# A layer pair with eight experts on one core: every expert ranked by load, none loaded ahead of the router

## The chip, the cores and the metric

The kernel runs on one core of one Trainium2 chip. The metric is the time of one launch on the device, in microseconds (us). The kernel before took 1318.35 us in the median of three runs (1315.09 to 1318.83). A profile is one further execution with the hardware profiler on; its span runs from the first to the last instruction.

## The reference, cut to what matters

Two layers are applied to 256 tokens of 1024 numbers (fp32): a mixer layer with a dense feed-forward, and a convolution layer with eight experts, of which each token takes two. Only the experts concern the change:

```python
def swiglu(u, w1, w3, w2):
    return (jax.nn.silu(u @ w1) * (u @ w3)) @ w2

logits = tokens @ router_w                    # 256 tokens, 8 experts
top_vals, top_idx = lax.top_k(logits, 2)
gates = jax.nn.softmax(top_vals, axis=-1)
# token by token: y = sum over its 2 experts e of gates[e] * swiglu(u, w1[e], w3[e], w2[e])
#   w1[e], w3[e]: 1024 x 2816, w2[e]: 2816 x 1024
x = x + gt_f * rmsnorm(y, ffn_post_g)
```

An expert's three matrices are 34.6 MB in fp32, all eight 277 MB. Each has to be read once, however few tokens its expert gets; how many it gets is known only when the router has run.

## The kernel before, in words

**Units.** All weights lie in memory as blocks of 128 x 2048 fp32 numbers, 1.05 MB each (a unit). An expert has 33: for each of five blocks of 512 hidden columns (j = 0 to 4) two units of w1, two of w3 and two of w2, and for the last 256 columns (j = 5) one of each. Eight experts have 264. A unit's key is `(name, expert, j, h)`; the same unit of the next expert lies `NU` = 33 further on. SP issues one transfer for a unit (or one for each half), and a transfer waits until the buffer that it goes to is free.

**Buffers.** The list `room` (L1557 to L1564) says, unit by unit, which buffers a unit goes to: six named `raw`, four pairs `whi`/`wlo`, one pair `gp`/`m`, three or four named `B`. A unit that goes to `whi`/`wlo` is one fp32 half in each; during a 128-slot expert these buffers hold something else (below), and the list goes round ten units instead of fifteen.

**Slots.** The token columns of an expert are gathered into slots by a one-hot matrix on TensorE (`Group.onehot`, `Group.gather`). How many slots an expert has is fixed when the program is built; which expert gets them is found at run time. The first turn is expert 0 with 96 slots (`FIRST`), and its addresses are known when the program is built. The other seven are ranked by their number of tokens (`ranks`, L1990), and rank r has `SLOTS[r]` slots out of 128, 96, 96, 96, 64, 64, 32. `TURNS` gives the order of work. So the slots of the eight turns are

| turn | 0 | 1 | 2 | 3 | 4 | 5 | 6 | 7 |
|---|---|---|---|---|---|---|---|---|
| before | 96 (expert 0) | 32 | 96 | 96 | 64 | 96 | 128 | 64 |

For the ranked ones SP reads the expert's base address from the tile `bases` into a register (L2054), and the transfers add it to a unit's place. An expert with more tokens than slots is finished in a loop after the last turn (`overflow`), whose count is also made in `ranks`.

**An expert's work.** For each j: `up` makes x·w1 and x·w3, `act` the gated product, `turn` transposes it on TensorE, and `down` multiplies by w2 into two PSUM banks; the downs of j - 1 stand behind the ups of j. With 128 slots (`Expert`) each weight half is split into a rounded and a remainder part (L372 on ACT, L373 on DVE, into the four `whi` and four `wlo`), and a product takes three matmuls of 128 x 512 in fp32r. With fewer (`Tiled`) fp32 weights are used as they are: a 64-slot pass puts two products side by side in TensorE's columns, a 32-slot pass four. 96 slots are one pass of each, and the units of w1 and w3 of one j stay in their buffers until the second pass is done. The last expert's result is scaled by its gates (`slot_gate`) and added on TensorE, the others on DVE.

**What sets the order.** From the last norm of the convolution layer on (L1707) the order of TensorE, DVE and ACT is that of the code (`in_order`). The list `todo` holds the expert steps; what stands in `due` (L2181 to L2218) is worked in between them: the rest of expert 0's gather, gates, ranks, and the one-hot and gather of the next group (`GROUPS`), which the turn before it carries. SP keeps the order in which loads are asked for, up to `AHEAD` steps ahead in the code and as far ahead in time as buffers allow. `warm(n)` is n matmuls whose result nobody reads.

**Steps ahead of the experts.** Norms, the transposes `turned` (L1718, L1721), the router's product `logits`, its two best per token `top2`, the places within an expert `slots` (a matmul with a triangle), `Group(0)`'s one-hot, the split token rows `parts` (L1598, L1599) and half of the first gather (L1748). Three units of expert 0 are asked for earlier still (L1542).

Of the kernel before, what the change touches and what calls it, by code (L numbers as in the profile page):

```python
# [236 lines left out]
def build(ctx: ExitStack, tc: tile.TileContext, d, unit, dbg=None):  # L237
# [1363 lines left out]
    def slots(t):  # L1601
# [5 lines left out]
        return lambda: V.tensor_copy(pos[:, t], pp[:, :NE])  # L1607

    def onehot(dst, iota_eq, selc):
        V.tensor_scalar(dst, K("iota"), iota_eq, selc, ALU.is_equal, ALU.mult)  # L1610

    def gather(Os, parts, hi_copy=A.copy, kps=range(KT // 2), bank="aux"):
# [4 lines left out]
        for kp in kps:  # L1617
# [6 lines left out]
            for a, b, dst in parts:  # L1624
# [5 lines left out]
                if len(dst) == 2:  # L1630
                    hi, lo = (x[:, 2 * kp : 2 * kp + 2] for x in dst)
                    hi_copy(hi, v)
                    V.tensor_tensor(lo, v, f(hi), ALU.subtract)
        return (i,)

    class Group:
# [61 lines left out]
    def slots_of(i):  # L1698
        return FIRST if TURNS[i] is None else SLOTS[TURNS[i]]
# [5 lines left out]
    place = {0: (lambda t: pos[:, t, 0:1], lambda t: sel[:, t, 0:1])}  # L1705

    with in_order():  # L1707
# [17 lines left out]
        A.copy(xT_[:, 4:8, P:], b1[1])  # L1725
        logits(0)
# [21 lines left out]
        i = g0.gather(range(2))  # L1748
# [86 lines left out]
    class Tiled(Expert):  # L1835
# [94 lines left out]
        def parts(self, g=None):  # L1930
# [3 lines left out]
            for on, p_, w, n in ((self.A, self.yp[0], 512, 1), (self.B, self.yp[1], T, 2)):  # L1934
# [37 lines left out]
    posr, selr, gtr = (tl([P, TT, NE - 1], n) for n in ("posr", "selr", "gtr"))  # L1972
    r7 = [tl([P, NE - 1, NE - 1], "r7", bufs=4) for _ in range(2)]
    bases = tl([P, NE - 1], "bases", I32)

    posv, selv, gtv = (tl([P, TT, 2 * NE], n) for n in ("posv", "selv", "gtv"))
    blocks = tl([P, 3, 8], "blocks", I32)

    def by_rank(dst, src):

        for t in range(TT):
            x = tl([P, NE - 1, NE - 1], "r7", bufs=4)
            G.tensor_tensor(x, r7[1], src[:, t, 1:].unsqueeze(1).to_broadcast([P, NE - 1, NE - 1]), ALU.mult)
            V.tensor_reduce(dst[:, t], x, AX.X, ALU.add)

# [4 lines left out]
    def ranks():  # L1990

        pcnt = pm("aux")
        for t in range(TT):
            mm(pcnt[:, 0:8], one, sel[:, t, :], t == 0, t == TT - 1)
        cnt, key = tl([P, NE], "cnt"), tl([P, NE], "key")
        A.copy(cnt, pcnt[:, 0:8])

        G.tensor_scalar(key, cnt, float(NE), None, ALU.mult)
        G.tensor_tensor(key, key, K("iota8"), ALU.subtract)
        sq = [P, NE - 1, NE - 1]  # L2000
        V.tensor_tensor(r7[0], key[:, 1:].unsqueeze(1).to_broadcast(sq), key[:, 1:].unsqueeze(2).to_broadcast(sq), ALU.is_gt)
        rank = tl([P, NE - 1], "rank")
        V.tensor_reduce(rank, r7[0], AX.X, ALU.add)
        i7 = K("iota8")[:, : NE - 1]
        V.tensor_tensor(r7[1], rank.unsqueeze(1).to_broadcast(sq), i7.unsqueeze(2).to_broadcast(sq), ALU.is_equal)
        x = tl(sq, "r7", bufs=4)
        G.tensor_tensor(x, r7[1], K("iota8")[:, 1:].unsqueeze(1).to_broadcast(sq), ALU.mult)
        b = tl([P, NE - 1], "bf")
        V.tensor_reduce(b, x, AX.X, ALU.add)
        V.tensor_scalar(bases, b, float(NU), None, ALU.mult)  # L2010
        by_rank(posr, pos)
        by_rank(selr, sel)

        cap = tl([P, NE], "cap")
        G.memset(cap, float(FIRST))
        G.memset(cap[:, 1:], float(P))
        for r in range(1, NE - 1):
            if SLOTS[r] != SLOTS[r - 1]:
                x = tl([P, NE - 1], "capx", bufs=2)
                V.tensor_scalar(x, rank, float(r), float(SLOTS[r - 1] - SLOTS[r]), ALU.is_ge, ALU.mult)  # L2020
                G.tensor_tensor(cap[:, 1:], cap[:, 1:], x, ALU.subtract)
        more = tl([P, 2 * NE], "more")
# [17 lines left out]
        V.tensor_copy(key, ti)  # L2040
        V.tensor_copy(blocks[:, 0], key)
        V.tensor_scalar(cnt, key, float(NE), float(NE), ALU.is_ge, ALU.mult)
        V.tensor_tensor(key, key, cnt, ALU.subtract)
        V.tensor_scalar(blocks[:, 1], key, float(NU), None, ALU.mult)
        V.tensor_scalar(top, top, 0.0, None, ALU.is_gt)
        V.tensor_reduce(key[:, 0:1], top, AX.X, ALU.add)
        V.tensor_copy(blocks[:, 2, 0:1], key[:, 0:1])

    base = []

    def at_base():

        for r in range(NE - 1):
            base.append(nc.values_load(bases[0:1, r : r + 1], engines=(ET.SP,), min_val=NU, max_val=(NE - 1) * NU))  # L2054
# [5 lines left out]
    sums_, gs = [], tl([P, 1], "gs")  # L2060
# [261 lines left out]
```

## Time and profile before

| what | us |
|---|---|
| median of three runs | 1318.35 |
| lowest, highest | 1315.09, 1318.83 |
| the profiled execution | 1315.59 |
| its span | 1313.5 |
| router's last choice written | 595.46 |
| first matmul of an expert starts | 604.62 |
| last matmul of the last expert ends | 1297.45 |

The profiled execution is 2.1 us longer than its span; the rest is launch. Times below count from the span's start. The experts take 693 of the 1313 us. In the tables of stretches, a stretch's columns are its length, then for each engine the busy time and the number of instructions, TensorE's granted clock (1.00 is 2.4 GHz, 0.50 is 1.2 GHz), the mean busy share of the DMA engines, and what they moved in GB/s. A busy TensorE is one with a matmul under way, at whatever clock.

### The profile page before, as it was taken

Reading aid. Unit: us, or ns where it says so; the run is one execution under the profiler, and the core shown is the slowest. Engines: PE = TensorE matmul, PEld = TensorE weight load, DVE = VectorE, ACT = ScalarE, POOL = GpSimd, SP = SyncE. Lnnn points to the kernel's source line nnn. Section 1 sums busy time; section 2 is a strip of 40 time slices with the busy share of each in tenths; the row PEclk is TensorE's granted clock in tenths of the full one; section 3 lists DMA queues with packets and bytes.
Section 4 is the critical chain, followed back from the end, with each engine's and each line's share of the span. In section 5 each row is a group of like instructions: output and inputs, shape, how many; then the busy total and the mean of one; then the engine's idle time right before and its main releaser. Section 6 shows DMA issues by size and latency. Waiting matters only on the chain. (4 is left out here: it accounts for less than half of the span.)

```text
span 1313.5 us, 22646 instructions
## 1 busy us (share of the span) xinstructions
PE 1249.1 (95%) x9212; PEld 803.6 (61%) x9212; DVE 641.1 (49%) x1065; ACT 439.2 (33%) x800; POOL 32.4 (2%) x83
## 2 busy tenths in 40 slices
PE   6999999989999998998999889999999999999996
PEld 5878777789998987675344333443433434678532
DVE  4589758698887658663202112011121121699422
ACT  4553246564434554253012000210011102577311
POOL 1000001100000010002000000000000000000000
PEclk8999999999999999987899889999999999999998
DMA  8727720478988616677679999999999996999994
GB/s 337 284 94 304 299 122 1 160 299 349 370 320 328 256 66 198 195 273 300 238 277 398 419 419 420 420 422 396 368 417 419 419 400 270 423 357 375 351 420 193
DMA packets 71090, 406.42 MB, mean 309 GB/s; under 512 B 7874, under 2 KB 12226, under 8 KB 31812
## 3 DMA queue, kind: packets, MB, share of 16 engines
q1 hardware_dynamic: 70980, 404.91, 78.8%
q8 instruction: 74, 1.21, 0.4%
q14 instruction: 36, 0.29, 0.1%
HBM read 402.94 MB, written 1.93 MB: 308 GB/s over the span
## 5 line engine op out<-in xcount | busy, mean ns | idle before, releaser
L373 DVE TENSOR_TENSOR wlo<-raw,whi 128x1024 fp32r<-128x1024 f32 x154 | 185.8, 1221 | 47.4 <-ACT whi L372 46.5
L282 PE MATMUL mm<-raw,gL 128*32 128x256 f32 (+3 forms) x1392 | 194.3, 438 | 5.1 <-DMA raw<-w 5.1
L372 ACT CAST whi<-raw 128x1024 fp32r<-128x1024 f32 x154 | 159.1, 1049 | 97.1 <-PE mm L282 61.2
L282 PE MATMUL mm<-B,whi 128*128 128x256 f32 x960 | 172.0, 282 | 0.2 <-issue 0.2
L282 PEld LDWEIGHTS mm<-B,whi 128*128 128x128 f32 x960 | 148.6, 189 | 2.3 <-issue 1.0
L282 PE MATMUL mm<-B,wlo 128*128 128x256 f32 x480 | 135.0, 281 | 0.0
L282 PE MATMUL mm<-B,gL 128*32 128x256 f32 (+3 forms) x808 | 124.4, 449 | 3.3 <-DMA B<-w 3.3
L282 PEld LDWEIGHTS mm<-raw,gL 128*32 128x32 f32 (+1 forms) x1392 | 76.8, 122 | 82.7 <-issue 57.3
L1887 DVE TENSOR_TENSOR cv<-cv,mm 64x512 f32<-64x512 f32 (+1 forms) x36 | 23.3, 647 | 189.9 <-ACT cv L1886 189.7
L1886 ACT ACTIVATE cv<-mm 64x512 f32<-64x512 f32 (+1 forms) x36 | 19.9, 553 | 268.1 <-PE mm L282 268.0
L282 PE MATMUL aux<-whi,pT 128*128 128x512 f32 (+2 forms) x400 | 100.9, 425 | 2.4 <-DVE pT L1903 1.8
L282 PEld LDWEIGHTS mm<-B,wlo 128*128 128x128 f32 x480 | 90.7, 189 | 0.0
L282 PEld LDWEIGHTS mm<-B,gL 128*32 128x32 f32 (+1 forms) x808 | 46.7, 123 | 55.4 <-issue 41.3
L282 PE MATMUL aux<-raw,pT 128*32 128x256 f32 (+1 forms) x592 | 77.9, 470 | 0.8 <-DMA raw<-w 0.8
L282 PE MATMUL aux<-wlo,pT 128*32 128x256 f32 (+2 forms) x284 | 69.4, 430 | 2.0 <-DVE wlo L373 1.1
L1903 DVE COPY pT<-aux 128x384 f32<-128x384 f32 (+4 forms) x42 | 19.0, 453 | 100.2 <-PE aux L1896 91.5
L282 PEld LDWEIGHTS aux<-whi,pT 128*128 128x128 f32 (+2 forms) x400 | 49.4, 158 | 27.3 <-issue 13.0
L282 PE MATMUL mm<-U,whi 128*128 128x256 f32 (+1 forms) x240 | 64.5, 331 | 0.0
L282 PE MATMUL aux<-B,pT 128*32 128x256 f32 (+2 forms) x424 | 59.7, 467 | 0.0
L282 PE MATMUL mm<-whi,gL 128*32 128x256 f32 (+3 forms) x336 | 55.9, 452 | 2.3 <-DMA whi<-w 2.3
L282 PE MATMUL mm<-whi,B 128*128 128x512 f32 (+1 forms) x192 | 57.9, 377 | 0.0
L282 PE MATMUL mm<-wlo,gL 128*32 128x256 f32 (+3 forms) x336 | 53.9, 445 | 0.2 <-DMA wlo<-w 0.2
(467 smaller groups left out, 1875.3 us busy)
## 6 DMA issues: line engine op xcount, KB each, us to landing
raw<-w SPq DMA_DIRECT2D x237, 1024.0 KB, 7.3
B<-w SPq DMA_DIRECT2D x69, 1024.0 KB, 11.2
whi<-w SPq DMA_DIRECT2D x52, 512.0 KB, 11.3
wlo<-w SPq DMA_DIRECT2D x52, 512.0 KB, 11.4
gp<-w SPq DMA_DIRECT2D x18, 512.0 KB, 10.0
m<-w SPq DMA_DIRECT2D x18, 512.0 KB, 10.0
B<-hd SPq DMA_DIRECT2D x24, 142.0 KB, 5.3
x<-x SPq DMA_DIRECT2D x2, 512.0 KB, 4.5
```

What stands on the lines that cost most here:

```text
L282: PE.matmul(out, lhsT, rhs, start=start, stop=stop)
L372: A.copy(hi, rq)
L373: V.tensor_tensor(lo, rq, f(hi), ALU.subtract)
L1886: A.activation(s, p_[:64, :w], AF.Silu)
L1887: V.tensor_tensor(s, s, p_[64:, :w], ALU.mult)
L1903: V.tensor_copy(h[:, :o], pt[:, :o])
```

## The change

All eight experts are ranked, and the slots of the eight turns become

| turn | 0 | 1 | 2 | 3 | 4 | 5 | 6 | 7 |
|---|---|---|---|---|---|---|---|---|
| after | 128 | 96 | 64 | 96 | 64 | 96 | 64 | 32 |

640 slots instead of 672: one 96 has become a 64. No unit of an expert is asked for before the bases are known. The count of tokens (`counted`) and the ranking (`ranks`) move from the first expert's work to the router, between `top2` and the gather; the ranking is done by MAX8 and FIND_INDEX8 instead of comparisons, and the sorted places come from one product and one sum over both token halves (`by_rank`). The part that counts leftovers is split (`too_many`, `left`) and stands later. Unselected tokens are now left out by place 0 instead of by a factor. 20 warm matmuls are added between the router's steps. The first four steps' units are loaded in two halves. The rounded part of the first gather is copied by DVE instead of ACT. Cut to its core:

```diff
-FIRST = 96
-SLOTS = (128, 96, 96, 96, 64, 64, 32)
-TURNS = (None, 6, 1, 2, 4, 3, 0, 5)
-GROUPS = ((0,), (1, 2), (3, 4), (5,), (6, 7))
+SLOTS = (128, 96, 96, 96, 64, 64, 64, 32)
+TURNS = (0, 1, 4, 2, 5, 3, 6, 7)
+GROUPS = ((0,), (1, 2), (3, 4), (5, 6), (7,))
...
-            if j:
-                for k in (("m1", 0, 0, 0), ("m3", 0, 0, 0), ("m1", 0, 0, 1)):
-                    pre[k] = raw(k)
...
-    room += ["raw"] * 3 + ["pT"] + ["w"] * 4 + ["xn", "gp"] + ["B8"] * 4
-    while asked() < whole - 30:
-        room += ["raw"] * 6 + ["w"] * 4 + ["gp"] + ["B8"] * 4
-    while asked() < whole + NU + 8:
-        room += ["raw"] * 6 + ["gp"] + ["B8"] * 3
-    while asked() < NU * NE - 13:
+    while len(room) < NU + 8:
+        room += ["raw"] * 6 + ["gp"] + ["B8"] * 3
+    while len(room) < NU * (NE - 1) - 6:
+        room += ["raw"] * 6 + ["w"] * 4 + ["gp"] + ["B8"] * 4
+    while len(room) < NU * NE - 13:
         room += ["raw"] * 6 + ["w"] * 4 + ["B8"] * 3
...
+    def counted():
+        pc = pm("mm")
+        for t in range(TT):
+            mm(pc[:, :NE], one, sel[:, t], t == 0, t == TT - 1)
+        return pc
+
+    def ranks(pc):
+
+        V.scalar_tensor_tensor(ckey, pc[:, :NE], float(NE), K("iota8"), ALU.mult, ALU.subtract)
+        V.max(top, ckey)
+        V.max_index(ti, top, ckey)
+        V.tensor_copy(tif, ti)
+        V.tensor_scalar(bases, tif, float(NU), None, ALU.mult)
+        V.tensor_tensor(r8, tif.unsqueeze(2).to_broadcast(sq), K("iota8").unsqueeze(1).to_broadcast(sq), ALU.is_equal)
...
+        warm(6)
         b0 = turned(xt[:, 0])
...
+        warm(3)
         b1 = turned(N.w[1])
...
+        warm(3)
         logits(0)
...
+        warm(2)
         logits(1)
...
+        warm(4)
         p0 = slots(0)
         top2(1, r1, ry)
+        warm(2)
+        pc = counted()
         p1 = slots(1)
+        ranks(pc)
...
-        i = g0.gather(range(2))
+        i = g0.gather(range(2), V.tensor_copy)
...
-            later(0, partial(g0.gather, (2, 3)))
-            later(1, gates, ranks)
-            later(2, g0.turn)
-            later(3, first)
+            later(2, *[partial(g0.gather, (k,), V.tensor_copy) for k in (2, 3)])
+            later(5, g0.turn)
+            later(7, gates, first, partial(by_rank, gtr, gt))
+            later(10, too_many)
+            later(30, left)
...
-                        if q == 0:
-                            r = raw(sk, src and src())
-                        halves_[key, q] = r[q] if few(key[1]) else half(r, q)
+                    if q == 0:
+                        r = raw(None, unit_of(key[1], key[0], *key[2:]), two=n < 4)
+                    halves_[key, q] = r[q] if few(key[1]) else half(r, q)
```

On SP, before, the first address is read (TENSOR_LOAD) behind 22 units of the first expert; the last of these are

```order
L347 DMA B_1131_6218<-w 128x2048
L347 DMA B_1132_6220<-w 128x2048
L347 DMA B_1169_6502<-w 128x2048
L347 DMA raw_6229<-w 128x2048
L347 DMA raw_6261<-w 128x2048
L347 DMA raw_6286<-w 128x2048
L347 DMA raw_6288<-w 128x2048
L2054 TENSOR_LOAD bases_5835
L2054 ISA x2
L347 DMA raw_1146_6336<-w 128x2048
```

On SP, of the change, it stands right behind the convolution's shifted rows (B from hd), ahead of every expert unit:

```order
L1347 DMA B_884_4576<-hd_5217 32x4x284 x4
L1347 DMA B_885_4577<-hd_5275 32x4x284 x4
L2049 TENSOR_LOAD bases_5682
L2049 ISA x2
L344 ISA
L344 DMA raw_5900<-w 128x1024
L344 ISA
L344 DMA raw_5900<-w 128x1024
L344 ISA
L344 DMA raw_5911<-w 128x1024
```

What moved is the address load: from behind 22 units of the experts to ahead of the first.

On DVE, before, from the router's last choice (sel) to the remainder of the token rows (B from x):

```order
L1594 SCALAR_TENSOR_TENSOR sel_5673<-cst_66,ixf_5678,s_1001_5672 128x8
L1607 COPY pos_5675<-mm_5776 128x8
L1663 TENSOR_SCALAR oh_5791<-cst_66,pos_5675,sel_5673 128x128 x2
L1599 SCALAR_TENSOR_TENSOR B_999_5670<-x_64,rs_1042_5738,B_998_5669 128x512
L1607 COPY pos_5675<-mm_5785 128x8
L1663 TENSOR_SCALAR oh_5791<-cst_66,pos_5675,sel_5673 128x128 x2
L1599 SCALAR_TENSOR_TENSOR B_999_5670<-x_64,rs_1048_5768,B_998_5669 128x512
```

On DVE, of the change, from the same choice to the first of these remainders:

```order
L1587 SCALAR_TENSOR_TENSOR sel_5667<-cst_66,ixf_5672,s_998_5666 128x8
L1714 SCALAR_TENSOR_TENSOR key_5681<-mm_5815,cst_66 128x8
L1715 MAX top_5678<-key_5681 128x8
L1716 MAX_INDEX ti_5679<-top_5678,key_5681 128x8
L1717 CAST tif_5680<-ti_5679 128x8
L1718 TENSOR_SCALAR bases_5682<-tif_5680 128x8
L1719 TENSOR_TENSOR r_1014_5683<-tif_5680,cst_66 128x64
L1601 SCALAR_TENSOR_TENSOR pos_5669<-mm_5803,sel_5667 128x8
L1601 SCALAR_TENSOR_TENSOR pos_5669<-mm_5818,sel_5667 128x8
L1725 TENSOR_TENSOR r8x_5833<-r_1014_5683,pos_5669 128x128
L1726 TENSOR_REDUCE posr_5684<-r8x_5833 128x16
L1608 TENSOR_SCALAR oh_5830<-iota_1008_5676,posr_5684 128x128
```

The ranking, ten instructions, now stands between the choice and the one-hot.

On PE, before, the router's matmuls stand back to back (aux: transposes; mm from rwg: logits):

```order
L575 MATMUL aux_5711<-cst_66,x_64 128x128 x4
L575 MATMUL aux_5716<-cst_66,x_64 128x128 x4
L575 MATMUL aux_5726<-cst_66,xn_5685 128x128 x4
L575 MATMUL aux_5731<-cst_66,xn_5685 128x128 x4
L282 MATMUL mm_5680<-rwg_5372,B_997_5668 128x8 x8
L282 MATMUL mm_5681<-rwg_5372,B_997_5668 128x8 x8
L282 MATMUL mm_5776<-sel_5673,cst_66 128x8
```

On PE, of the change, the warm matmuls (from identr) stand between them, and the count (sel, one) behind the places of the first half:

```order
L281 MATMUL mm_5715<-identr_522 128x512 x6
L574 MATMUL aux_5722<-cst_66,x_64 128x128 x4
L574 MATMUL aux_5727<-cst_66,x_64 128x128 x4
L281 MATMUL mm_5737<-identr_522 128x512 x3
L574 MATMUL aux_5741<-cst_66,xn_5689 128x128 x4
L574 MATMUL aux_5746<-cst_66,xn_5689 128x128 x4
L281 MATMUL mm_5758<-identr_522 128x512 x3
L281 MATMUL mm_5674<-rwg_5372,B_994_5662 128x8 x8
L281 MATMUL mm_5777<-identr_522 128x512 x2
L281 MATMUL mm_5675<-rwg_5372,B_994_5662 128x8 x8
L281 MATMUL mm_5798<-identr_522 128x512 x4
```

Fourteen of the warm ones stand ahead of the second half's logits, six more ahead of the count.

## Rows read from the trace of the kernel before

**Rows 1.** The page's busy times: engine, us, share of the span, instructions.

```profile
PE 1249.1 (95%) x9212; PEld 803.6 (61%) x9212; DVE 641.1 (49%) x1065; ACT 439.2 (33%) x800; POOL 32.4 (2%) x83
```

**Rows 2.** Stretches: router with loads ahead, then one row an expert, then the end.

```profile
544.00:600.00 56.00, 52.41 (x356) 41.59 (x355) 35.21 (x90) 25.14 (x55) 4.01 (x9) 0.88 0.83 284
600.00:701.45 101.45, 96.21 (x806) 44.10 (x810) 15.20 (x55) 16.78 (x41) 5.50 (x28) 0.93 0.71 276
701.45:761.65 60.20, 49.35 (x675) 24.75 (x677) 10.88 (x23) 5.55 (x13) 0.00 (x0) 0.89 1.02 421
761.65:860.01 98.36, 94.92 (x827) 40.67 (x823) 15.19 (x31) 13.09 (x33) 0.00 (x0) 0.98 1.02 419
860.01:954.65 94.64, 94.64 (x885) 39.13 (x887) 15.58 (x28) 8.49 (x18) 0.00 (x0) 1.00 0.98 394
954.65:1027.94 73.29, 73.29 (x461) 29.32 (x461) 14.00 (x27) 10.21 (x22) 0.00 (x0) 1.00 1.02 419
1027.94:1121.83 93.89, 93.89 (x804) 39.61 (x804) 16.03 (x31) 14.07 (x35) 0.00 (x0) 1.00 0.89 360
1121.83:1221.99 100.16, 99.52 (x549) 76.27 (x547) 86.91 (x85) 73.55 (x82) 0.00 (x0) 1.00 0.97 378
1221.99:1291.72 69.73, 69.16 (x341) 29.02 (x341) 17.85 (x26) 11.25 (x20) 0.00 (x0) 1.00 0.98 398
```

**Rows 3.** Timeline of ACT: activations of the last column block, first and last expert.

```profile
701.45 0.38 ACT L1886 ACTIVATE cv<-mm 64x256 f32<-64x256 f32 x1 [7.40 <-PE mm L282]
...
1291.72 0.38 ACT L1886 ACTIVATE cv<-mm 64x256 f32<-64x256 f32 x1 [7.37 <-PE mm L282]
```

**Rows 4.** Timeline of SP: the last loads ahead, and the next ones.

```profile
591.87 3.55 SPq L347 DMA_DIRECT2D B<-w  x5
615.00 20.70 SPq L347 DMA_DIRECT2D raw<-w  x6
```

**Rows 5.** Timeline of PE and DVE in the router and at the first expert.

```profile
581.51 6.32 PE L282 MATMUL aux<-B,B 128*128 128x512 f32 x27
595.23 0.23 DVE L1594 SCALAR_TENSOR_TENSOR sel<-cst,ixf,s 128x8 f32<-128x8 f32 x1
595.57 0.60 DVE L1663 TENSOR_SCALAR oh<-cst,pos,sel 128x128 fp32r<-128x128 f32 x2
595.97 0.57 PE L282 MATMUL mm<-sel,one 128*128 128x8 f32 x2
597.47 2.07 DVE L1599 SCALAR_TENSOR_TENSOR B<-x,rs,B 128x512 fp32r<-128x512 f32 x3
604.62 12.08 PE L282 MATMUL mm<-raw,gL 128*64 128x512 f32 x96
```

**Rows 6.** Timeline of DVE: MAX8 to the cast of what it found.

```profile
623.97 0.18 DVE L2038 MAX8 top<-more 128x8 f32<-128x16 f32 x1 [3.04 <-POOL more L2035]
624.46 0.17 DVE L2040 CAST key<-ti 128x8 f32<-128x8 uint32 x1
```

**Rows 7.** The address loads, and a stretch behind the load issued at 615.00.

```profile
L2054 SPq TENSOR_LOAD <-bases x7: 262/265/459, 619.7 to 661.3; - x7
...
617.00:618.00 1.00, 1.00 (x9) 0.69 (x10) 0.00 (x0) 0.39 (x2) 0.38 (x2) 1.00 1.00 401
```

**Rows 8.** The page's group of remainder subtractions on DVE.

```profile
L373 DVE TENSOR_TENSOR wlo<-raw,whi 128x1024 fp32r<-128x1024 f32 x154 | 185.8, 1221 | 47.4 <-ACT whi L372 46.5
```

**Rows 9.** Timeline of PE: two w2 units at 64 slots, then the end.

```profile
1282.88 3.60 PE L282 MATMUL aux<-raw,pT 128*64 128x512 f32 x16
1293.60 3.85 PE L282 MATMUL aux<-raw,pT 128*64 128x512 f32 x16
```

**Rows 10.** Stretches of the clock, from the router to the first expert's end.

```profile
595.00:604.60 9.60, 8.94 (x38) 8.51 (x38) 4.43 (x12) 2.26 (x6) 0.31 (x2) 0.50 1.01 407
...
626.56:632.00 5.44, 5.44 (x20) 2.11 (x22) 0.68 (x4) 0.00 (x0) 0.00 (x0) 0.56 0.02 6
632.00:701.45 69.45, 69.45 (x648) 31.00 (x648) 8.79 (x19) 9.78 (x26) 0.00 (x0) 1.00 0.76 288
```

More of the change, by code (lines that the diff above doesn't have):

```diff
@@ L1606, in slots, with onehot @@
             mm(pp[:, :NE], one, sel[:, 0], False, True)
[L1607 to L1610 removed]
+        return lambda: V.scalar_tensor_tensor(pos[:, t], pp[:, :NE], 1.0, sel[:, t], ALU.add, ALU.mult)
+    iota1 = tl([P, P], "iota1")
+    G.tensor_scalar(iota1, K("iota"), 1.0, None, ALU.add)
+    def onehot(dst, place, w=P, a=0):
+        src = iota1[:, a : a + w].unsqueeze(1).to_broadcast([P, P // w, w])
+        V.tensor_scalar(dst.rearrange("p (n c) -> p n c", c=w), src, place, None, ALU.is_equal)
     def gather(Os, parts, hi_copy=A.copy, kps=range(KT // 2), bank="aux"):
@@ L1698, in slots_of, with by_rank @@
     def slots_of(i):
-        return FIRST if TURNS[i] is None else SLOTS[TURNS[i]]
+        return SLOTS[TURNS[i]]
     def few(i):
         return slots_of(i) < P
-    place = {0: (lambda t: pos[:, t, 0:1], lambda t: sel[:, t, 0:1])}
+    top, ti, tif = tl([P, NE], "top"), tl([P, NE], "ti", U32), tl([P, NE], "tif")
+    ckey, bases = tl([P, NE], "key"), tl([P, NE], "bases", I32)
+    sq = [P, NE, NE]
+    r8 = tl(sq, "r8")
+    posr, gtr = tl([P, TT, NE], "posr"), tl([P, TT, NE], "gtr")
+    def counted():
[10 more added lines that the diff above has]
+        V.tensor_tensor(r8, tif.unsqueeze(2).to_broadcast(sq), K("iota8").unsqueeze(1).to_broadcast(sq), ALU.is_equal)
+    def by_rank(dst, src):
+        s4 = [P, TT, NE, NE]
+        x = tl(s4, "r8x")
+        V.tensor_tensor(x, r8.unsqueeze(1).to_broadcast(s4), src.unsqueeze(2).to_broadcast(s4), ALU.mult)
+        V.tensor_reduce(dst, x, AX.X, ALU.add)
     with in_order():
@@ L1970, in gates @@
             V.scalar_tensor_tensor(gt[:, t, :], s1[:, t, :], gg[:, t, 1:2], gt[:, t, :], ALU.mult, ALU.add)
[L1972 to L1984, printed above, removed]
@@ L1987, in build @@
     side = tl([P, 2], "side")
     V.tensor_reduce(side, ident.rearrange("p (a b c) -> p b a c", a=2, b=2), AX.XY, ALU.add)
[L1990 to L2022, printed above, removed]
@@ L2023, in ranks, with too_many @@
+    posv, gtv = (tl([P, TT, 2 * NE], n) for n in ("posv", "gtv"))
+    blocks = tl([P, 3, 8], "blocks", I32)
+    cap, cnt, more = tl([P, NE], "cap"), tl([P, NE], "cnt"), tl([P, 2 * NE], "more")
+    def too_many():
+        for r, w in enumerate(SLOTS):
+            if r == 0 or w != SLOTS[r - 1]:
+                G.memset(cap[:, r:], float(w))
+        G.tensor_tensor(cnt, top, tif, ALU.add)
+        G.tensor_scalar(cnt, cnt, 1.0 / NE, None, ALU.mult)
         for n in range(2):
@@ L2035, in ranks, with left, at_base @@
                 G.tensor_scalar(more[:, c], more[:, c], float(NE), None, ALU.subtract)
-        top, ti = tl([P, 8], "top"), tl([P, 8], "ti", U32)
+    def left():
         V.max(top, more)
         V.max_index(ti, top, more)
[L2040 to L2044, printed above, removed]
-        V.tensor_scalar(top, top, 0.0, None, ALU.is_gt)
[L2046 to L2054, printed above, removed]
+        V.tensor_copy(tif, ti)
+        V.tensor_copy(blocks[:, 0], tif)
+        V.tensor_scalar(cnt, tif, float(NE), float(NE), ALU.is_ge, ALU.mult)
+        V.tensor_tensor(tif, tif, cnt, ALU.subtract)
+        V.tensor_copy(blocks[:, 1], tif)
+        V.tensor_scalar(top, top, 0.0, None, ALU.is_gt)
+        V.tensor_reduce(ckey[:, 0:1], top, AX.X, ALU.add)
+        V.tensor_copy(blocks[:, 2, 0:1], ckey[:, 0:1])
+    base = {}
+    def at_base(r):
+        if r not in base:
+            base[r] = nc.values_load(bases[0:1, r : r + 1], engines=(ET.SP,), min_val=0, max_val=(NE - 1) * NU)
+        return base[r]
     dbg("gt", gt)
@@ L2084, in overflow @@
                 q = nc.values_load(blocks[0:1, 0, bass.ds(i, 1)], min_val=0, max_val=2 * NE - 1)
-                at = nc.values_load(blocks[0:1, 1, bass.ds(i, 1)], engines=(ET.SP,), min_val=0, max_val=(NE - 1) * NU)
+                r = nc.values_load(blocks[0:1, 1, bass.ds(i, 1)], engines=(ET.SP,), min_val=0, max_val=NE - 1)
+                at = nc.values_load(bases[0:1, bass.ds(r, 1)], engines=(ET.SP,), min_val=0, max_val=(NE - 1) * NU)
                 block(at, q)
```

49 lines of the change are left out of this document (16 added, 33 removed).

## The prediction, on record before the changed kernel ran

> **What bounds the kernel now.** I read the page's busy times first: PE is busy 95% of the span, DVE 49%, ACT 33% [rows 1]. That average hides stages, so next came the stretches cut at each expert's last activation, the first at 701.45 and the last at 1291.72 us [rows 2, 3]. The reader is to see three things in them.
>
> - From 761.65 on PE is busy nearly without a gap at clock 0.98 to 1.00. A turn of 96 slots costs 94 to 98 us, one of 64 73.3 or 69.7, the one of 128 100.2.
> - The turn of 32 is different: PE is busy 49 of 60.2 us, while the DMA engines are full (share 1.02, 421 GB/s). It waits for weights.
> - Elsewhere DMA is full only now and then: 276 GB/s in the first expert, 394, 360, 378 and 398 later, where it waits for buffers. Full speed is 419 GB/s, so a unit (1.049 MB) takes 2.50 us, an expert's 33 units 82.6 us and all 264 units 661 us.
>
> So light turns are paid for in weights, heavy ones in matmuls, and what decides is the lead: how many units have landed beyond those that PE needs at the end of a turn. It follows from rows 2: in the 32 turn 421 GB/s for 60.2 us is 24.2 units against 33 used, and PE waits at its end, so the lead there is near 0; I put it at 2, units that landed while PE did its last block. Then the next turns land 39.3, 35.6, 29.3, 32.2, 36.1 and 26.5 units, and the lead is 8.3, 10.9, 7.2, 6.4, 9.5 and 3.0. The most that the fifteen-unit buffers held is about 10.9, the ten-unit ones about 9.5.
>
> The head start before: 15.9 MB (15.2 units) moved from 544 to 600 [rows 2]. Then SP issued nothing between 595.4 and 615.0 [rows 4], since buffers were full, and the first expert ran at 276 GB/s.
>
> **The change, step by step.** All against the profiled execution: span 1313.5, time 1315.6.
>
> 1. *Warm matmuls.* One costs 6.32 / 27 = 0.234 us [rows 5]. Fourteen stand ahead of the second logits, 3.3 us at full clock. PE is the late one there (its product ends at 587.8 and the transposes follow at once), so I take 3.1 us; the bounds are 0 (all in waits for ACT) and 6.6 (half clock). The last choice, written at 595.46 before [rows 5], comes at 598.6.
> 2. *Count and ranking.* Two matmuls of the kind that took 0.57 us [rows 5], with handoffs 0.7: 599.3. Then a product from PSUM (0.25), MAX8 to the cast (623.97 to 624.63 = 0.7 [rows 6]) and the bases (0.3): 600.6. SP's load of a base took 0.46 at the first, with register work some 0.7. From a load's issue at 615.00 the stream needed until 617 to be full [rows 7], so its full speed starts 2 us after the bases: 602.6.
> 3. *First matmul.* DVE still has the rest of the ranking and the sorted places (five small operations, 1.3 us, estimated from the 0.2 to 0.3 us of its neighbours), then one-hots and remainders, which took from 595.57 to 599.54, 4.0 us [rows 5]: 605.9. The gather, its copy to two parts by DVE, and the first weight's remainder (1.22 us [rows 8]) follow. I put the first expert's steady start at 609.5, against 604.62 [rows 5]: 4.9 us later. Bounds: 606 (only step 2 counts) and 615.
> 4. *Turns 0 to 6.* Turn 0 (128): 100.2 us, less 11 for the tail of another turn that this stretch holds (three w2 units of 96 slots at 2.7 and what adds it back, estimated at 3), plus 3.8 for a gather of two experts (98.4 against 94.6), plus 5 for its own late gather and a cold, thinly fed start: 98. DVE is the near bound there, busy 86.9 of 100.2 us. Turn 1 (96): 94.6. Turns 2 and 4 (64 behind 96): 73.3 and 0.7 for the second expert in the gather, 74 each. Turns 3 and 5 (96 behind 64): 94.6 less 2.6, since the tail is three units of 64 at 1.8 us [rows 9] instead of 2.7: 92 each. Turn 6: 73.3. Sum 597.9, so turn 6 ends at 609.5 + 597.9 = 1207.4.
> 5. *Turn 7 (32).* Its matmuls are the cheapest, so weights pace it. The lead: turn 0 alone could land (707.5 - 602.6) / 2.5 = 42 units, 12 more than used, but ten-unit buffers hold 9.5. Turn 1 adds nothing (its first seventeen units still go round ten): 9.5. Then 74 us land 29.6 (6.1), 92 us 36.8 (9.9), 6.5, 10.3, and 73.3 us 29.3: 6.5 at 1207.4. Three units of turn 6 and all of turn 7 are 36; 29.5 have still to land: 74 us, the last at 1281.2. PE needs 2 us behind it.
> 6. *The end.* From PE's last w2 product, 1297.45, to the span's end are 16.05 us [rows 9]. The last expert's 32-slot parts are four short operations in place of two long ones, beside a product that already takes as long: +0.5. The span is 1281.2 + 2 + 16.5 = 1299.7, the time 1301.8, 13.8 us less. Bounds of step 5: a lead of 13 (no stall) or of 0, at 2.5 us a unit, 1285 to 1318.
>
> In sum, the start is 4.9 later, and the experts with the end are shorter by 18.7. Smaller edits (gates, `too_many` and `left` on POOL and DVE later, the one-hot without its factor) lie beside PE's work in turn 0; each costs DVE under 2 us, which is late only if DVE becomes the bound there, priced in the 98. Before, the ranking stood inside turn 0, and the clock was at 0.56 from 626.56 to 632 [rows 10]; that goes.
>
> The three timed runs lie from 0.5 below to 3.2 above the profiled execution; I add 1.2 and predict 1303.
>
> By the reference's own router the experts get 98, 82, 78, 70, 60, 55, 51 and 18 tokens, which fit the new slots, so the leftover loop stays empty.
>
> **A rule that speaks against it.** The trace before had 15.2 units in place when the first expert began, and the change gives them up [rows 2]. The Trainium skill, "DMA: Bandwidth & Descriptors", section "Rules for kernel authors", says to issue a transfer early and wait for it late. That is the first rival below. By the rows DMA was idle for 67 us between 600 and 1291 (101 us at 276 of 419, 95 at 394, 94 at 360, 100 at 378, 70 at 398), so lost early transfers can be made up later as long as buffers allow.
>
> **Rivals.**
>
> - *The head start is lost in full.* Were DMA the bound throughout, 15.2 units at 2.5 us would come on top: 1315.6 + 38 = 1354. For it: the last turn is paced by weights. Against: those 67 us, more than 38. It decides once less than 25 of them can be used. 4%.
> - *The lead collapses (slower).* A light turn uses 33 units in 74 us and lands 29.6, so it must begin with 3.7 units of lead. With ten buffers at the beginning, and 96-slot turns that hold four w1 and w3 units until their second pass, the lead might stay at 3 or less. Then turn 7 begins with none and needs 36 x 2.5 = 90 us: 1207.4 + 90 + 18.5 = 1316, time 1318, and each light turn below 3.7 adds up to 9 more: 1318 to 1336. It is slower than before from a lead of 0 at turn 6's end. For it: 360 GB/s in the turn ahead of 128, where the list had shrunk. Against: the 64 turn at 419 GB/s with PE never waiting. 10%.
> - *The clock stays low in turn 0.* In the router the granted clock was 0.50 [rows 10], the lower of its two levels, 1.2 GHz, and the new start feeds PE thinly. The Trainium skill, "TensorE: Matmul & The Clock Gate", section "HAM oscillation — how this bites in real kernels", tells of a kernel in which each wait for DMA made PE start cold again. Here the clock was back at 1.00 from 632 on [rows 10]. At half clock a half unit takes 2.8 us for PE and 1.25 for DMA, so PE is never idle, which is what preceded the recovery at 626 to 632. Each us at half clock costs half of one; for no gain it needs 26 us. 5%: 1315 to 1330.
> - *No stall at all.* If buffers hold 13 units, the last one lands at 602.6 + 661 = 1263.6, and the time is 1263.6 + 18.5 + 2.1 = 1284. For it: DMA needs only 661 of the 695 us. Against: rows 2 show less than full speed in every 128 turn and in 96 behind 96. 13%.
>
> **How the numbers follow.** My forecast, 1303, has 68% and its own range is 1292 to 1315. Within 0.3% (4 us, about what three runs that differ by 3.7 us can tell) means 1314.4 to 1322.3. Faster: the forecast nearly whole (0.64) and no stall (0.13), 0.76. Same: 0.10, half from the collapse just at its point. Slower: 0.14. The range 1287 to 1318 leaves out most of the no-stall case below and the rivals above.
>
> **What would show it.** Step 2: bases written near 600.6, DMA full from 603. Step 3: the first expert matmul near 609. Step 4: turns of 98, 95, 74, 92, 74, 92, 73 us with PE busy throughout. Step 5: DMA at 419 GB/s from turn 5's end to the last unit, PE waiting in turn 7 alone, which lasts about 70 us. Step 6: 18 us from the last landing to the end. I am wrong if PE waits in a 64 turn, if turn 0 takes over 105 us, or if the last unit lands before 1268 or after 1295.

## The result, and the profile after

The changed kernel takes 1329.36 us in the median of four runs (1327.92 to 1331.30), the kernel before 1316.92 beside it: 1.0105 times the time, 95% interval 1.0083 to 1.0127. It is slower by 1.05%, and the forecast was 1303. Its profiled span is 1327.9 us.

The page's busy times, which answer to [rows 1], show PE less busy, by 14.5 us, in a span that is 14.4 us longer:

```profile
PE 1234.6 (93%) x8655; PEld 793.5 (60%) x8655; DVE 635.7 (48%) x1055; ACT 432.9 (33%) x786; POOL 33.1 (2%) x72
```

The stretches, cut as in [rows 2]: the router, then one row a turn, then the end. The last activations of the first and the last turn, where they are cut, stand below.

```profile
544.00:604.80 60.80, 58.74 (x429) 45.35 (x421) 37.09 (x99) 25.13 (x53) 4.26 (x9) 0.92 0.13 33
604.80:716.49 111.69, 100.53 (x474) 82.32 (x475) 90.46 (x116) 81.38 (x104) 5.14 (x15) 0.92 0.93 372
716.49:809.72 93.23, 93.23 (x788) 41.41 (x790) 17.97 (x27) 9.69 (x18) 0.00 (x0) 1.00 0.86 345
809.72:883.50 73.78, 73.78 (x463) 29.55 (x463) 14.14 (x29) 12.89 (x32) 0.00 (x0) 1.00 1.02 416
883.50:973.16 89.66, 89.66 (x768) 36.52 (x768) 13.29 (x23) 6.36 (x13) 0.00 (x0) 1.00 1.02 416
973.16:1046.94 73.78, 73.78 (x463) 29.55 (x463) 14.14 (x29) 12.89 (x32) 0.00 (x0) 1.00 1.02 417
1046.94:1141.76 94.82, 91.01 (x768) 35.80 (x768) 13.29 (x23) 6.37 (x14) 0.00 (x0) 1.00 1.02 417
1141.76:1216.18 74.42, 73.59 (x460) 29.30 (x459) 13.36 (x25) 9.60 (x23) 0.00 (x0) 1.00 1.02 417
1216.18:1305.00 88.82, 56.49 (x570) 23.76 (x569) 11.40 (x23) 7.00 (x16) 0.00 (x0) 0.85 0.93 380
1305.00:1327.90 22.90, 8.04 (x59) 4.88 (x51) 7.82 (x16) 4.68 (x13) 1.12 (x2) 0.71 0.23 88
```

```profile
716.49 0.38 ACT L1809 ACTIVATE cv<-mm 128x256 f32<-128x256 f32 x1
...
1305.00 0.27 ACT L1916 ACTIVATE cvt<-mm 64x128 f32<-64x128 f32 x1 [9.84 <-PE mm L281]
```

Read the last column first. From turn 2 to turn 6 DMA moves 416 to 417 GB/s whatever the turn, light or heavy: it never pauses. In [rows 2] it paused in five of eight turns. So from about 770 us on the end was set by the weights, and PE, which looks full until turn 6, was working off its lead. In the last turn the lead is gone, and PE waits 32 of 88.8 us. All eight turns hold 652 us of PE work (the PE column added up), against 671 before. A unit of 1.049 MB at 417 GB/s takes 2.52 us, so all 264 are 664 us: more than PE's work. Before, 249 units were still to land at 600, 623 us at 2.50 each, against 671: there PE was the longer one by 48 us.

Smaller stretches show where DMA did pause, behind the turn of 128 and near the end:

```profile
690.00:716.50 26.50, 26.47 (x149) 22.52 (x148) 22.04 (x20) 22.25 (x31) 0.00 (x0) 1.00 0.82 314
716.50:740.00 23.50, 23.50 (x160) 12.75 (x160) 8.44 (x11) 5.82 (x10) 0.00 (x0) 1.00 0.61 237
740.00:770.00 30.00, 30.00 (x256) 11.68 (x252) 5.62 (x9) 1.93 (x4) 0.00 (x0) 1.00 0.86 341
...
1270.00:1280.00 10.00, 6.78 (x54) 2.35 (x54) 2.84 (x6) 2.17 (x5) 0.00 (x0) 0.69 0.67 276
1280.00:1290.00 10.00, 4.69 (x32) 1.52 (x32) 0.00 (x0) 0.00 (x0) 0.00 (x0) 0.67 0.58 223
```

Against 417 GB/s that is 6.5 + 10.1 + 5.5 us lost in the first three rows and 8.0 in the last two. In the first three, units of turn 1 still went round ten buffers: up to 716 SP waited 16.4 us for DVE's remainders of turn 0, behind that mostly for PE, 11.8 us at the longest, whose 96-slot passes held w1 and w3. The last two are a single load on SP: the third B buffer of the last turn is the first one's, so SP, which keeps its order, stood still until the first load had landed (9.0 us) and PE had finished with it at 1283 (5.3 us more).

```profile
1266.32 1.72 SPq L346 DMA_DIRECT2D B<-w  x2
...
1283.11 0.34 SPq L346 DMA_DIRECT2D B<-w  x1
```

The start, in the order of the prediction's steps (DVE's last choice and the bases, SP's first load, ACT, DVE, PE):

```profile
600.44 0.23 DVE L1587 SCALAR_TENSOR_TENSOR sel<-cst,ixf,s 128x8 f32<-128x8 f32 x1
603.62 0.17 DVE L1718 TENSOR_SCALAR bases<-tif 128x8 int32<-128x8 f32 x1
604.79 2.02 SPq L344 DMA_DIRECT2D raw<-w  x4
608.77 1.04 ACT L371 CAST whi<-raw 128x1024 fp32r<-128x1024 f32 x1 [10.24 <-DMA raw<-w]
612.65 1.04 ACT L371 CAST whi<-raw 128x1024 fp32r<-128x1024 f32 x1 [2.13 <-DMA raw<-w]
613.61 0.80 ACT L1627 ACTIVATE cvt<-aux,modc,gain 128x128 f32<-128x128 f32 x2
615.31 4.62 DVE L372 TENSOR_TENSOR wlo<-raw,whi 128x1024 fp32r<-128x1024 f32 x4
616.58 0.80 PE L281 MATMUL mm<-wlo,B 128*128 128x512 f32 x1 [4.88 <-DVE wlo L372]
```

The gather's second pair of activations (613.61) stood on ACT behind a cast that waited until 612.65 for the second half unit; DVE's copy and the first remainder follow it, and PE runs nearly without gaps from 616.58.

### The profile page after: what moved, and what is told of

Its sections match the earlier page's. It is cut to its first block, busy times and chain, and to the rows that moved or that the text cites. A ratio compares the mean times of both kernels' runs of the same rounds, so it can differ in the third digit from the quotient of the medians.

```text
span 1327.9 us, 21579 instructions
## 1 busy us (share of the span) xinstructions
PE 1234.6 (93%) x8655; PEld 793.5 (60%) x8655; DVE 635.7 (48%) x1055; ACT 432.9 (33%) x786; POOL 33.1 (2%) x72
## 5 line engine op out<-in xcount | busy, mean ns | idle before, releaser
L281 PE MATMUL mm<-raw,gL 128*32 128x256 f32 (+3 forms) x1200 | 185.8, 461 | 13.6 <-DMA raw<-w 11.4
L281 PE MATMUL mm<-B,whi 128*128 128x256 f32 x960 | 174.7, 283 | 0.2 <-DVE B L631 0.2
L281 PEld LDWEIGHTS mm<-raw,gL 128*32 128x32 f32 (+1 forms) x1200 | 69.5, 125 | 89.7 <-issue 56.7
L281 PE MATMUL aux<-raw,pT 128*32 128x256 f32 (+1 forms) x584 | 73.0, 463 | 5.9 <-DMA raw<-w 3.7
L281 PE MATMUL aux<-wlo,pT 128*128 128x512 f32 (+2 forms) x244 | 68.2, 456 | 1.4 <-DVE wlo L372 1.1
L281 PEld LDWEIGHTS aux<-raw,pT 128*32 128x32 f32 (+1 forms) x584 | 25.2, 119 | 47.7 <-issue 37.7
## 6 DMA issues: line engine op xcount, KB each, us to landing
m<-w SPq DMA_DIRECT2D x17, 512.0 KB, 10.1
```

The source lines that it names most:

```text
L281: PE.matmul(out, lhsT, rhs, start=start, stop=stop)
```

## The experiments

Ratios are to the kernel before in runs on the same chip, with their 95% intervals; a ratio of 0.01 is 13 us. The first theory was that of the section above (A, weights) against one in which PE's late, cold start and its unbroken work set the end (B).

**Buffers.** `e1_ring40` starts the list of fifteen at the 41st unit.

```diff
-    while len(room) < NU + 8:
+    while len(room) < NU:
```

> The fifteen-unit list of buffers starts at the 41st unit instead of the 51st. Theory A (weights): in the changed kernel the DMA engines were full from 770 to 1270 us, so the end is set by what they lost before and after; between 690 and 770 they lost about 22 us because units of turn 1 still went round ten buffers. Then this edit gives back 10 to 15 us: 1314 to 1319 us, with DMA at 400 GB/s or more from 716 to 770 (237 and 341 before). Theory B (PE): PE was busy without a gap from 716 to 1130, so weights landing sooner only wait in buffers: no change, within 3 us of 1329.

Measured: 1.0016 (0.9998 to 1.0033), 1318.0 us. Theory A's range. The stretch behind 740 is full; the one ahead of it, which theory A had at 400 too, is nearly as in the changed kernel:

```profile
716.00:740.00 24.00, 24.00 (x161) 11.15 (x159) 5.75 (x8) 4.41 (x7) 0.00 (x0) 1.00 0.61 246
740.00:770.00 30.00, 30.00 (x282) 12.40 (x282) 6.17 (x10) 1.93 (x4) 0.00 (x0) 1.00 1.02 409
```

`e2_tail0` takes the B buffers out of the end of the list, `e3_both` does both, `e4_nowarm` removes the warm matmuls of the router: the twenty, and two more that the kernel before has as well.

```diff
-        room += ["raw"] * 6 + ["w"] * 4 + ["B8"] * 3
+        room += ["raw"] * 6 + ["w"] * 4
```

```diff
-        warm(6)
         b0 = turned(xt[:, 0])
...
-        warm(2)
         pc = counted()
```

> The last 31 units use only the six raw buffers and the four whi/wlo pairs; the B buffers are left out of the list there. The third B load of the last turn was issued 15 us after the second, at the moment at which PE had done with the first, and DMA fell to 276 and 223 GB/s between 1270 and 1290: 8 us lost. Theory A: the hole goes and the end comes 7 to 9 us earlier, 1320 to 1322 us. Theory B, or if ten buffers are too few with so little lead: within 3 us of 1329.

> Both list edits together. Theory A: they add up, since both give DMA idle time back: 18 to 23 us less than the changed kernel, 1306 to 1311 us, which is below the kernel before by 6 to 11. Theory B: within 3 us of 1329. If the lead that the first edit makes already fills the hole at the end, the sum is that of the first alone, 1314 to 1319.

> The changed kernel without its 20 warm matmuls in the router. Theory A: the bases are written 3 us earlier and so is everything behind them, since the first units set turn 0 and turn 0 sets when buffers come free: 2 to 4 us less, 1325 to 1327. Rival: the warm matmuls keep the clock up and the first matmuls of turn 0 run at 0.50 longer without them: 0 to 4 us more, 1329 to 1333.

Measured: 1.0047 (1.0028 to 1.0065), 1.0012 (0.9997 to 1.0026) and 1.0066 (1.0044 to 1.0088). The hole at the end costs 7.6 us by itself, but the two edits don't add up: where weights land sooner, the hole is smaller already (373 and 321 GB/s from 1270 to 1290 in `e1_ring40`, 276 and 223 after). Of the 11.7 us between `e1_ring40` and the changed kernel, the stretch behind 740 gives 4.9 and the smaller hole 4.7; `e3_both` closes the rest of the hole (419 and 408) without a gain beyond the intervals. By the two ratios the warm matmuls cost 5 us, give or take 4; what they may give the clock doesn't make up for it.

`f4_combo` went further: fifteen buffers from the 31st unit, ten at the end, no warm matmuls.

```diff
-    while len(room) < NU + 8:
+    while len(room) < NU - 3:
...
```

> The changed kernel with the fifteen-unit list from the 31st unit on, ten buffers for the last 31 units, and without the warm matmuls. Theory A: of the 10 us of DMA time that the version with the list from the 41st unit still lost between 716 and 740, half comes back, the warm matmuls give 3 to 4: 1306 to 1312 us. If the whi/wlo pairs are not free before turn 0 ends, so that a load waits for them and all behind it, the longer list gives nothing or costs: 1313 to 1318.

Measured: 1.0104 (1.0087 to 1.0120). The second alternative, and worse. The loads for whi/wlo wait on SP until the turn of 128 lets these go, with all loads behind them:

```profile
690.00:716.00 26.00, 25.97 (x142) 21.93 (x141) 22.45 (x23) 21.93 (x29) 0.00 (x0) 1.00 0.42 163
```

**Slots and head start.** `f1_first64` is the slot cut alone, in the kernel before; `f3_nohead` the head start alone taken away (the three units asked for earliest join the list); `f2_head` the head start given back to the changed kernel.

```diff
-FIRST = 96
+FIRST = 64
```

```diff
-            if j:
-                for k in (("m1", 0, 0, 0), ("m3", 0, 0, 0), ("m1", 0, 0, 1)):
-                    pre[k] = raw(k)
...
+        V.tensor_scalar(zero, sel[:, 1, 0:1], 0.0, None, ALU.mult)
         p1 = slots(1)
...
-            return key, None
+            if not late:
+                late.append(nc.values_load(zero[0:1, 0:1], engines=(ET.SP,), min_val=0, max_val=(NE - 1) * NU))
+            return None, lambda: unit_from(late[0], key)
```

```diff
-                        r = raw(None, unit_of(key[1], key[0], *key[2:]), two=n < 4)
+                        r = raw((key[0], 7, *key[2:]), unit_of(key[1], key[0], *key[2:]) if key[1] else None, two=n < 4)
```

> The kernel before with 64 slots instead of 96 for its first expert: 640 slots as in the changed kernel, with the early loads and the order of before. Theory A (weights decide, and the head start is kept): the first turn needs some 20 us less of PE, but between 600 and 762 us only 51 units have to land, which at 2.53 us each is 129 us, so most of the gain stays: 10 to 20 us less than before, 1297 to 1307. Rival: the turn of 32 behind it then waits for its weights as much longer, since buffers and not DMA held the first turn at 276 GB/s: no gain, 1313 to 1317.

> The kernel before, whose first expert's loads read their address from a tile that is written behind the router's last choice (the value is always 0): the head start taken away, nothing else. A1: DMA had idle time to make up for it, 34 us between 601 and 701 alone, and the turn of 32 waits a little longer: 2 to 10 us more than before, 1319 to 1327. A2: 15.2 units at 2.53 us, 38 us more, 1350 to 1356.

> The changed kernel with its first expert's place in memory fixed when the program is built (it is the expert with the most tokens in this input), so that its units need not wait for the router: the head start given back, nothing else. Theory A1 (the ten-unit list holds the lead at about 9 whenever turn 0 ends): the head start is lost again by the end of turn 0, and only the first matmuls come earlier, by the 5 to 8 us for which they waited for weights: 1321 to 1325. Rival A2 (the units not loaded ahead are what the change lost): 10 units at 2.53 us come on top, 25 us less: 1300 to 1307.

Measured: 0.9824 (0.9809 to 0.9838), 1292.1 us; 1.0033 (1.0020 to 1.0046), 1318.8; 1.0102 (1.0084 to 1.0121), 1329.5. So the slot cut by itself is worth 23 us, above the range of its expectation. Taking away the head start costs the kernel before only 4. In the changed kernel giving it back brings nothing, less than the 5 to 8 us expected. Its ten-unit list had room for only seven units ahead of the router (DMA moved 133 GB/s from 560 to 600), so this run gives back a part of the head start and not the whole; with the list full DMA then ran below 310,

```profile
632.00:660.00 28.00, 25.94 (x109) 21.01 (x110) 24.56 (x25) 21.11 (x23) 1.50 (x4) 0.94 0.85 309
660.00:690.00 30.00, 27.71 (x125) 22.32 (x124) 23.81 (x37) 20.20 (x26) 0.00 (x0) 0.94 0.87 306
```

and turn 0 ended at 717.99, where without the head start it ended at 716.49.

**The order.** These three left 37 us between two kernels of 640 slots. I took the order of turns for it (theory C): `g1_order` gives the changed kernel the order of before, the list that goes with it, and the places in the first turn at which the rest of the first gather stood before. `g2_light2` moves only the turn of 32, `g3_heavy2` puts the turn of 128 second in `f1_first64`, `g4_swap12` exchanges two turns there.

```diff
-TURNS = (0, 1, 4, 2, 5, 3, 6, 7)
-GROUPS = ((0,), (1, 2), (3, 4), (5, 6), (7,))
+TURNS = (4, 7, 1, 2, 5, 3, 0, 6)
+GROUPS = ((0,), (1, 2), (3, 4), (5,), (6, 7))
...
```

```diff
-TURNS = (0, 1, 4, 2, 5, 3, 6, 7)
+TURNS = (0, 7, 1, 4, 2, 5, 3, 6)
```

```diff
-TURNS = (None, 6, 1, 2, 4, 3, 0, 5)
-GROUPS = ((0,), (1, 2), (3, 4), (5,), (6, 7))
+TURNS = (None, 0, 1, 4, 2, 6, 3, 5)
+GROUPS = ((0,), (1,), (2, 3), (4, 5), (6, 7))
```

```diff
-TURNS = (None, 6, 1, 2, 4, 3, 0, 5)
+TURNS = (None, 1, 6, 2, 4, 3, 0, 5)
```

> The changed kernel (all eight ranked, nothing ahead of the router, warm matmuls) with only the order of its turns and the list of buffers that goes with it as before: 64, 32, 96, 96, 64, 96, 128, 64 slots. Theory C (the order decides: DMA loses its time while the turn of 128 holds the whi/wlo buffers, and at the start and the end of the list there is no slack to make up for it): the version of before with 640 slots, 1292, plus 3 for the head start and 2 to 6 for the later bases: 1296 to 1302 us. Theory D (the longer router and the missing head start decide, whatever the order): 1318 to 1330.

> The changed kernel with its turn of 32 slots moved from the last place to the second: 128, 32, 96, 64, 96, 64, 96, 64. Theory C: the turn of 32 frees buffers as fast as units land, so the 15 us that DMA lost between 716 and 770 go, and the lead lost in it is regained in turns of 96: turn 1 ends near 784, 500 us of turns follow, 1300 to 1308. Theory D, or if PE's wait in the turn of 32 is only moved from the end to the start: 1322 to 1330.

> The kernel before with 640 slots (64 for its first expert) and the turn of 128 second: 64, 128, 96, 64, 96, 32, 96, 64. By the account of DMA time, some 72 units have landed when the turn of 128 ends near 780, and 192 at 2.53 us follow, 485 us; with 5 to 15 lost behind the turn of 128 and 18 at the end: 1288 to 1302 us. If a turn of 128 near the start costs by itself what the changed kernel lost: 1312 or more.

> The kernel before with 640 slots and the turns of 32 and 96 behind the first exchanged: 64, 96, 32, 96, 64, 96, 128, 64. In the version with 32 second PE waited for weights some 21 us between 690 and 760; here a turn of 96 goes ahead in which the buffers fill to a lead of 8 to 11, so the turn of 32 waits 8 us less or more: 1282 to 1288 us. If the head start had given that lead already, no change: 1290 to 1294.

Measured: 1.0078 (1.0050 to 1.0107), 1328.3 us; 1.0027 (1.0011 to 1.0044), 1320.6; 0.9859 (0.9834 to 0.9884), 1297.8; 0.9746 (0.9721 to 0.9770), 1282.5. Theory C fell as it stood: with the order of before the changed kernel is as slow as with its own, and a turn of 128 near the start costs little where there is a head start. `g2_light2` lies between the two expectations, and its DMA paused again near its end (286 and 15 GB/s from 1260 to 1280). In `g1_order` DMA is full from 620 to 900 while PE waits for it:

```profile
620.00:900.00 280.00, 237.65 (x1948) 98.68 (x1944) 37.95 (x89) 31.76 (x76) 0.00 (x0) 0.96 1.02 416
```

`g4_swap12` is the fastest of all and beats both kernels: a turn of 96 behind the first lets a lead build up before the turn of 32 uses it. That turn, from activation to activation, in `f1_first64` and then in `g4_swap12`:

```profile
679.23:741.78 62.55, 45.99 (x558) 21.81 (x558) 8.59 (x18) 3.43 (x8) 0.00 (x0) 0.86 1.02 420
```

```profile
761.71:824.43 62.72, 52.11 (x714) 27.98 (x715) 12.51 (x29) 11.81 (x32) 0.00 (x0) 0.97 1.01 421
```

PE waits 10.6 us there instead of 16.6. These 6 us are the order's part of the 10 between the two kernels that the traces show; in the same two executions the router's last choice comes 4.8 us sooner in `g4_swap12` (593.19 for 598.03) with the same code up to there, and why is not shown.

**What the head start is worth at 640 slots.** Open was whether that or the longer router made the difference (theory E or not). `h1_64_nohead` is `f3_nohead` with `FIRST = 64`; `h2_order_head` is `g1_order` with its first expert fixed, by the edit of `f2_head` with 0 for 7.

> Both edits to the kernel before: 64 slots for its first expert (640 in all) and that expert's loads behind the router's last choice. Theory E (what the head start is worth depends on the slots: with 672 PE's work hides the weights, with 640 it does not): 13.5 units at 2.53 us are 34 us; DMA can make up the 11 us that it idled between 600 and 660 and a part of what it idles behind 840: 1308 to 1320 us, 16 to 28 more than with the head start. Rival F (a head start costs 3 us wherever it is taken away, as in the kernel before): 1293 to 1300.

> The version of the changed kernel with the turns in the order of before (64, 32, 96, 96, 64, 96, 128, 64), and its first expert's place in memory fixed when the program is built (it is expert 0 in this input): the head start given back to a turn whose list has fifteen buffers. Theory E: 1328 less 28 to 36, 1292 to 1300 us. Rival: the longer router, the warm matmuls or the ranking ahead of the gather made that version slow: 1318 to 1328.

Measured: 1.0012 (0.9999 to 1.0025), 1317.6 us, and 0.9911 (0.9895 to 0.9926), 1303.6. The first is as theory E has it, the second lies 4 us above its range and far below the rival's. From 600 to 760, without the head start and then with it (`f1_first64`), PE has 124 us of work done or 135, with DMA full in the first:

```profile
600.00:760.00 160.00, 124.10 (x842) 52.53 (x845) 21.17 (x68) 17.98 (x43) 5.51 (x28) 0.88 1.02 415
```

```profile
600.00:760.00 160.00, 134.80 (x1052) 60.28 (x1053) 24.67 (x75) 19.77 (x47) 5.53 (x28) 0.89 0.95 387
```

Where the time goes is seen at the last activations of turn 0 and of the turn of 32 behind it, without the head start, in `h1_64_nohead` and then in `f3_nohead`:

```profile
680.20 0.38 ACT L1885 ACTIVATE cv<-mm 64x256 f32<-64x256 f32 x1 [7.93 <-PE mm L282]
...
763.37 0.27 ACT L1885 ACTIVATE cvt<-mm 64x128 f32<-64x128 f32 x1 [10.68 <-PE mm L282]
```

```profile
703.16 0.38 ACT L1885 ACTIVATE cv<-mm 64x256 f32<-64x256 f32 x1 [7.40 <-PE mm L282]
...
764.99 0.27 ACT L1885 ACTIVATE cvt<-mm 64x128 f32<-64x128 f32 x1 [9.60 <-PE mm L282]
```

Turn 0 is 23 us shorter at 64 slots, and yet the turn of 32 ends at nearly the same time: 166.5 and 168.5 us after the first load (167.6 in `g1_order`), and the 66 units of two turns take 166 us at 2.52. Without the head start the weights set this end, whatever the slots. With it the turn of 32 ends at 741.78 (`f1_first64`), 21.6 us sooner (24 when each is counted from its router's last choice), but at 761.65 in the kernel before, only 3.3 us sooner. What follows takes 550 to 554 us in all four, with PE waiting under 1 us from 800 to 1270, and there DMA pauses again without any use for it:

```profile
760.00:1300.00 540.00, 534.07 (x3934) 258.56 (x3928) 166.18 (x230) 131.18 (x208) 0.00 (x0) 0.99 0.97 390
```

So the ratios, less 1, in percent:

| | head start | none | none, and the change's router | head start, and the change's router |
|---|---|---|---|---|
| 672 slots | 0 | +0.33 | | |
| 640, order of before | -1.76 | +0.12 | +0.78 | -0.89 |
| 640, order of the change | | | +1.05 | +1.02 (seven units) |

In the order of before the head start costs 0.33% to lose at 672 slots and 1.88% at 640 (25 us; 1.67% by `g1_order` against `h2_order_head`). One way from before to the changed kernel is then -1.76 (slots), +1.88 (head start), +0.66 (router and ranking ahead of the first load, issued at 604.7 in `g1_order` where `h1_64_nohead` has 596.9, with all else of the change that stands there) and +0.27 (order), of which the last is within the intervals of its two kernels. Another way has the same ends and other parts: -1.76 (slots), +0.87 (router, `h2_order_head`), +1.91 (order with its list, `f2_head`) and +0.03 (head start). So the lost head start and the order with its ten-unit list each cost 1.9% where they are counted first and nearly nothing where they are counted second; they can't be fully parted, since that list cuts a head start to seven units. The list matters without a head start too: `e1_ring40` gives back 11.7 us.

## Why the prediction was wrong, step by step

- *Steps 1 and 2* were late by 2.1 and 3.2 us: the last choice at 600.67 for 598.6, the bases at 603.79 for 600.6. Step 2 left out the two warm matmuls that stand ahead of the count, 1.2 us at clock 0.50. The first load was issued at 604.79, where I had DMA full from 602.6.
- *Step 3* failed in size, and beyond its bounds: PE ran steadily from 616.58, not 609.5 (606 to 615). I had the gather and the first weight side by side; on ACT and DVE they stood in one queue, and each cast that waited for weights held up the gather's activation.
- *Step 4* was right in its durations: turn 0 took 99.9 us from its start (98 forecast), the others 93.2, 73.8, 89.7, 73.8, 94.8 and 74.4 (94.6, 74, 92, 74, 92, 73.3), where 94.8 holds 3.8 of waiting. Turn 6 ended at 1216.2 for 1207.4: 7.1 us of step 3's error and 1.7 of the turns.
- *Step 5* is the one that failed. Turns 0 to 6 landed 39.6, 30.7, 29.3, 35.6, 29.3, 37.7 and 29.6 units (GB/s by length), so with the prediction's own count the leads were 9.6, 7.3, 3.6, 6.1, 2.5, 7.2 and 3.8, for 9.5, 9.5, 6.1, 9.9, 6.5, 10.3 and 6.5. "Turn 1 adds nothing" was wrong by 2.2 units, which stayed missing to the end: the forecast had those seventeen units go round ten buffers and yet land at PE's pace, and left out of its sum that a turn of two passes holds w1 and w3 until the second, which only a rival mentions. The last turn took 88.8 us, not about 70. PE's last w2 product began at 1309.24, and step 5 had the last unit at 1281.2: 28 us, of which 7.6 are the later end of turn 1, 5.5 the 2.2 units, 8.0 the hole behind 1270. Some 7 are left: a unit at 2.515 us and not 2.50 is 2.8 of them (0.6% of 460 us), the rest I can't divide. Counted from the first load the 28 us come out whole: it was issued 2.2 after 602.6, 264 units take 664 us and not 661, and DMA lost 40.4 us up to 1309.24, where step 5 holds 17.6 (1281.2 less the 1263.6 of *no stall*), so 22.8 more. The lost head start is no error on top of these: step 5 counts every unit from 602.6 on.
- *Step 6* was right: 18.7 us from there to the end, for 18.5.

PE's last products, which answer to [rows 9], each behind a wait for weights:

```profile
1306.64 1.07 PE L281 MATMUL aux<-raw,pT 128*32 128x256 f32 x16 [0.62 <-SPq L2079]
1309.24 1.07 PE L281 MATMUL aux<-raw,pT 128*32 128x256 f32 x16 [1.53 <-SPq L2079]
```

The rivals. The time lies in the range of *the lead collapses* (1318 to 1336, given 10%), and its mark, a small lead when turn 7 begins, is what the trace shows (3.8); but the light turns didn't wait for weights as it had it, only turn 5 for 3.8 us. *The head start is lost in full* (4%) named one of the two causes, and I argued it away wrongly. Of the 67 us of idle DMA time that were to make up for it [rows 2], only the 35 in turn 0 lay ahead of the turn that waits for weights. `f3_nohead` shows that they were nearly enough for the kernel before. The slot cut took 23 us out of just that turn, and `h1_64_nohead` shows that the pauses behind it are of no use. The price was 25 us and not 38, since with the head start DMA still paused in the first turns (387 GB/s from 600 to 760, without it 415). In the order of the change the rival fails as far as it was tried: the seven units of `f2_head` bring nothing. The Trainium skill's rule that I weighed there ("DMA: Bandwidth & Descriptors", section "Rules for kernel authors": issue early, wait late) agrees with the runs at 640 slots in the order of before (25 us), and hardly matters at 672 (4 us) or in `f2_head`.

*The clock stays low* was not it: PE was at 0.50 from 604.8 to 616.58, where it mostly waited, and at 1.00 from 632 on.

```profile
604.80:616.58 11.78, 5.02 (x18) 3.98 (x18) 5.94 (x13) 5.45 (x8) 3.63 (x11) 0.50 0.88 308
616.58:632.00 15.42, 15.42 (x65) 12.76 (x66) 11.94 (x14) 9.45 (x15) 0.00 (x0) 0.83 1.02 421
632.00:660.00 28.00, 25.93 (x115) 20.66 (x114) 25.73 (x33) 22.59 (x25) 1.50 (x4) 1.00 1.01 420
```

What stays open: how the 0.66% of the router divide between the warm matmuls, the ranking and the rest, and why the router's time differs from execution to execution of the same code. Its last choice comes at 600.44 to 603.93 in eight profiles of the changed router (`f2_head` has the latest), and at 593.19 to 598.03 in four of the one before, so a few us between two profiles prove nothing; the ratios rest on several runs. The version of `g4_swap12` with all experts ranked wasn't tried, nor a whole head start in the order of the change.

## What to carry to other kernels

Before counting idle time of one engine as room for lost early work, put the work on each engine side by side as the change leaves it, turn by turn from the start and not only in sum: only idle time ahead of the turn that waits can make up for anything. Two edits that cost 4 us and gain 23 one by one can together gain nothing, so price them together. Where buffers are handed out in a fixed list, look for the unit whose buffer is held longest. Here a turn of 96 ahead of the lightest one also saved PE 6 us of waiting.

## What the runs showed of the hardware that was not expected

Loads issued close together don't land one after another: eight were issued from 604.79 to 610, four of them half units, and ACT had the first half at 608.77 and the second only at 612.65, though 0.52 MB take 1.26 us at 417 GB/s. By then DMA had moved 1.9 MB (246 GB/s from 604.80 to 612.65), nearly twice the 1.05 MB of these two halves.
